# Scores, decay, rate and gate as plain 32-bit products on half the array's height, in a hybrid attention and RWKV layer

## Chip, cores, metric

The kernel runs on one core of one Trainium2 chip. The metric is device time in microseconds for one launch. The core's engines are TensorE (PE, with its weight loads as PEld), VectorE (DVE), ScalarE (ACT), GpSimd (POOL) and SyncE (SP, which issues most DMAs). Every engine works through its own instructions in order and waits on semaphores for the others.

## What is computed

One decoder layer on 512 positions with 16 learned positions ahead of them (528 in all), width 1024, all in 32 bits. After a layer norm, one projection gives the inputs of two branches and their gates. One branch is attention over a sliding window of 128 positions with 16 query heads and 2 key heads of width 64; the other is a recurrent time mixing (RWKV-7) with 16 heads. The parts of the reference that the change touches:

```python
proj = h @ w_in[l]
q, k, v, zr, gate_att, gate_rwkv = jnp.split(proj, [c0, c1, c2, c3, c4], axis=-1)
...
logits = jnp.einsum('nqkgd,nskd->kgnqs', qb, kw).astype(jnp.float32) * (HEAD_DIM ** -0.5)
...
w = -jax.nn.softplus(-(w0 + jnp.tanh(wl) @ w2)) - 0.5      # decay
a = jax.nn.sigmoid(a0 + al @ a2)                           # rate
g = jax.nn.sigmoid(gl) @ g2                                # output gate
...
merged = jax.nn.sigmoid(gate_att) * att + jax.nn.sigmoid(gate_rwkv) * rw
h = layer_norm(ALPHA * h + merged @ w_out[l], ln1_g[l], ln1_b[l])
ff = jnp.square(jax.nn.relu(h @ w_ff1[l])) @ w_ff2[l]
h = layer_norm(ALPHA * h + ff, ln2_g[l], ln2_b[l])
```

`decay_w2` and `iclr_a2` have 64 rows, `gate_w2` 128; a head's query and key have width 64, so the scores are sums over 64 values.

## The kernel before

Activations lie with channels on the 128 partitions and positions along the free dimension. A large product is made of split operands: a 32-bit number x becomes a high part hi (rounded to the type fp32r) and a low part lo = x - hi. ACT makes hi by a copy, DVE makes lo by a subtraction (`split`, lines 256 and 259, for weights), and the helper `three` (lines 339 to 342) adds hi·hi, hi·lo and lo·hi into one PSUM bank.

The first 560 us or so interleave the two branches; then follow the output projection and the two feed-forward products. The heads go in 8 pairs (index j), each on 128 partitions, 64 for each head. Two kinds of work are woven on TensorE. A *unit* is a column block of the projection, made by `dense` in steps (8 steps of 512 positions, or 16 of 264), each step three products. All else is an *item* with a due time. `weave` keeps a clock that each dense step advances by a fixed estimate, 3 x (0.014 + n / 2400) us for n positions (0.372 for 264, 0.682 for 512; line 371), and puts an item into TensorE's order as soon as the clock has reached its time. TensorE's order is fixed by this; the other engines' orders come from the framework's scheduler with priorities (`ahead`). Stage s of the loop at line 1447 scans pair s, solves pair s - 1, projects decay and rate of pair s + 1 (`project_in`, items at 7.4 and 8.6), makes the scores of pair s - 1 (`attend`) and the attention output of pair s - 2. In the middle stages the units are the two gates (512 positions each), then keys and reads (264), the query (512) and the values (264).

Around the change:

- `low_rank` and `gate_rank` make the shared inputs: `zw` and `za` hold hi on partitions 0 to 63 and lo on 64 to 127 for decay and rate; `sghi` and `sglo` hold the gate's.
- `rwkv_begin` loads a pair's 64-row weights of decay and rate, laid out twice, below each other, and splits them. `rwkv_lora(j, 0)` makes decay for both halves of the positions and `rwkv_lora(j, 1)` the rate: for each half one product with the weights' hi (against hi and lo of the input at once, 128 rows) and one with lo. Each half takes one PSUM bank and is read by a tanh on ACT (line 500). After decay follow a scan on DVE (line 505) and exponentials on ACT (lines 512 to 516), which the pair's keys use.
- `aside_query` splits the query (`qhi` by ACT, line 1073; `qlo` by DVE, line 1074) and moves the parts by four DMAs into `qs`, with hi and lo of one head below each other. `aside_key` and `aside_heads` do the like for the key, with each head's hi twice, and lo twice.
- `attention_scores(j, n)` makes the scores of query block n of 128 against 256 keys for both heads in one bank: two products for each head, with the key's hi and lo. DVE then merges the window's two halves and adds the bias (lines 1140, 1141). It is called four times for a pair, at t0, t0, t0 + 2.8 and t0 + 4.4, and the last call also does the softmax.
- `gate_out` makes the output gate with `three`; DVE multiplies it into the other gate (line 1126).

Small products such as decay and rate, gate, scores, and the softmax's transposes (`pt`) and attention output (`av`) share the PSUM pool `pat` with two banks, used in turn; the dense steps have another with two banks (`dn`).

Other small products already take plain 32-bit operands: `rwkv_scores` (line 668) and `rwkv_fold` (line 890) use 64 rows, one head after the other on the two halves of the array; `rwkv_turn_inverse` (line 873) uses all 128 rows; the chain of states (line 950) uses all rows and half of the columns. On the planner's clock `rwkv_fold` has its items at 8.4 and 10.6, `rwkv_turn_inverse` at 6.4, the chain one each 0.95 from 11.6, `gate_out` 11.6.

Of the kernel before, what the change touches and what calls it, by code (L numbers as in the profile page):

```python
# [11 lines left out]
F32 = mybir.dt.float32  # L12
# [72 lines left out]
ABUF = {'qs': 1, 'ga': 1, 'gg': 1, 'pa': 1, 'z': 1, 'bv': 1}  # L85
# [45 lines left out]
def hybrid_layer_kernel(ctx: ExitStack, tc: tile.TileContext, I: dict, out: bass.AP):  # L131
# [298 lines left out]
    zw = lz.tile([P, T], F32R, name="zw", tag="zw")  # L430
    za = lz.tile([P, T], F32R, name="za", tag="za")
    sghi = lz.tile([P, SEQ], F32R, name="sghi", tag="sghi")
    sglo = lz.tile([P, SEQ], F32R, name="sglo", tag="sglo")
# [11 lines left out]
    def low_rank(zl):  # L445
        twl = ew.tile([HD, T], F32, name="twl", tag="u")
        act.activation(twl, zl[0:HD], AF.Tanh)
        tal = ew.tile([HD, T], F32, name="tal", tag="L")
        act.copy(tal, zl[HD:P])
        for dst, src in ((zw, twl), (za, tal)):  # L450
            act.copy(dst[0:HD], src)
            dve.tensor_tensor(dst[HD:P], src, dst[0:HD].bitcast(F32), op=ALU.subtract)

    def gate_rank(zg):
        sg = ew.tile([P, SEQ], F32, name="sg", tag="v")
        act.activation(sg, zg[:, NMETA:], AF.Tanh, scale=0.5)
        dve.tensor_scalar(sg, sg, 0.5, 0.5, op0=ALU.mult, op1=ALU.add)
        act.copy(sghi, sg)
        dve.tensor_tensor(sglo, sg, sghi.bitcast(F32), op=ALU.subtract)
# [16 lines left out]
    def rwkv_begin(j):  # L476

        S = SS[j]
        lw = ew.tile([P, 2, P], F32, name="lw", tag="lw")
        lhi = ew.tile([P, 2 * P], F32R, name="lhi", tag="lhi")  # L480
        llo = ew.tile([P, 2 * P], F32R, name="llo", tag="llo")
        lf = lw.rearrange("p a c -> p (a c)")
        nc.sync.dma_start(lf, I["lora"][j])
        act.copy(lhi, lf)
        dve.tensor_tensor(llo, lf, lhi.bitcast(F32), op=ALU.subtract)
        S["lora"] = lhi, llo
# [3 lines left out]
    def rwkv_lora(j, q):  # L490
        S = SS[j]
        lhi, llo = S["lora"]
        zz, dst, bias = ((zw, S["tw"], "w0h"), (za, S["ta"], "a0h"))[q]
        qc = slice(q * P, (q + 1) * P)
        for t0, n in ALLT:
            ps = pat.tile([P, 512], F32, name="dps", tag="a")
            ts_ = slice(t0, t0 + n)
            pe.matmul(ps[:, :n], lhi[:, qc], zz[:, ts_], start=True, stop=False)
# [1250 lines left out]
```

## Time and profile before

| | |
|---|---|
| median of 3 runs | 990.89 us (987.24 to 992.4) |
| profiled execution: its time, its span | 988.82 us, 986.7 us |
| mean granted clock of TensorE | 0.994 |
| PE, PEld | 943.9, 790.8 us busy |
| DVE, ACT, POOL | 654.9, 455.0, 45.9 us busy |
| DMA | 105.46 MB, mean 107 GB/s |

The profile is of one execution. In the timeline a row is start (us), duration (us), engine, line, operation, tiles written<-read, rows*columns of the array for TensorE, shapes, and in brackets the idle time ahead of it with what ended it. TensorE's products overlap, so that their durations (0.28 us for 264 columns) exceed the distance of their starts (0.12 us); what a product costs is that distance. A 32-bit product appears as two instructions. Group rows give busy us, mean ns, and after the bar the idle time before them.

### The profile page before, as it was taken

What the parts mean: (1) busy time and instruction counts of PE and PEld (TensorE: products, weight loads), DVE (VectorE), ACT (ScalarE), POOL (GpSimd) and SP (SyncE); (2) the same over time, 40 slices, a digit from 0 to 9 for tenths busy, and PEclk for the clock granted to TensorE, in tenths of its full rate; (3) what the DMA queues carried; (4) which work ended last, traced back from release to release, by engine and by line L of the source; (5) the groups of instructions that cost most, each with busy time, mean ns of one, the idle gap of its engine ahead of it and who ended that gap; (6) DMA issues with size and microseconds to landing.
All of it is one profiled execution on the core that took longest, in us unless ns stands there. A gap on an engine that the chain in (4) does not pass through costs nothing.

```text
span 986.7 us, 19121 instructions
## 1 busy us (share of the span) xinstructions
PE 943.9 (96%) x7557; PEld 790.8 (80%) x7557; DVE 654.9 (66%) x1505; ACT 455.0 (46%) x1130; POOL 45.9 (5%) x108
## 2 busy tenths in 40 slices
PE   4999999999999999999999999999999999999996
PEld 3889878788888887888876778888888888888885
DVE  8677887888887888778786967666523244452427
ACT  6635447465473664654726834644412133442220
POOL 2000000010010000100001001000000000000001
PEclk9999999999999999999999999999999999999998
DMA  7545323233324432242534536133232323223222
GB/s 272 95 131 150 90 73 105 82 77 98 91 74 120 105 98 59 69 111 80 147 116 105 194 114 228 44 122 113 89 103 86 106 86 104 89 88 104 76 96 85
DMA packets 82673, 105.46 MB, mean 107 GB/s; under 512 B 47766, under 2 KB 54664, under 8 KB 82584
## 3 DMA queue, kind: packets, MB, share of 16 engines
q1 hardware_dynamic: 81088, 102.16, 35.0%
q10 hardware_dynamic: 1496, 2.08, 0.6%
q8 instruction: 59, 0.97, 0.4%
q14 instruction: 30, 0.25, 0.1%
HBM read 86.29 MB, written 13.74 MB: 101 GB/s over the span
## 4 chain that ended last, share of the span: by engine, by line
PE 72%; DVE 16%; ACT 5%; DMA 3%; issue 2%; POOL 2%; SPq 0%; DVEq 0%; ACTq 0%; POOLq 0%
PE dps L340 12%; PE dps L341 11%; PE dps L342 11%; PE acc L1518 6%; PE acc L1520 6%; PE acc L1519 6%; DVE wlo L259 3%; DMA wraw<-in_w_in_dram 2%; PE sc L668 2%; PE o L1292 1%; PE av L1196 1%; PE wp L873 1%; POOL grs L973 1%; PE ch L950 1%; PE o L1293 1%
## 5 line engine op out<-in xcount | busy, mean ns | idle before, releaser
L259 DVE TENSOR_TENSOR wlo<-wraw,whi 128x512 fp32r<-128x512 f32 x240 | 158.4, 686 | 178.2 <-ACT whi L256 177.4
L256 ACT CAST whi<-wraw 128x512 fp32r<-128x512 f32 x240 | 140.5, 616 | 271.8 <-PE dps L341 131.2
L340 PE MATMUL dps<-hhi,whi 128*128 128x264 f32 (+1 forms) x640 | 217.7, 340 | 7.3 <-DVE qlo L1074 5.5
L341 PE MATMUL dps<-hlo,whi 128*128 128x264 f32 (+1 forms) x640 | 204.5, 320 | 1.1 <-DVE hlo L321 1.1
L342 PE MATMUL dps<-hhi,wlo 128*128 128x264 f32 (+1 forms) x640 | 204.1, 319 | 0.4 <-DVE wlo L259 0.4
L340 PEld LDWEIGHTS dps<-hhi,whi 128*128 128x128 f32 x640 | 121.5, 190 | 22.2 <-DVE qlo L1074 6.8
L342 PEld LDWEIGHTS dps<-hhi,wlo 128*128 128x128 f32 x640 | 121.4, 190 | 9.1 <-DVE wlo L259 0.6
L341 PEld LDWEIGHTS dps<-hlo,whi 128*128 128x128 f32 x640 | 121.8, 190 | 7.3 <-DVE hlo L321 1.9
L341 PE MATMUL dps<-h1lo,whi 128*128 128x512 f32 (+1 forms) x256 | 97.5, 381 | 0.0
L340 PE MATMUL dps<-h1hi,whi 128*128 128x512 f32 (+1 forms) x256 | 97.5, 381 | 0.0
L342 PE MATMUL dps<-h1hi,wlo 128*128 128x512 f32 (+1 forms) x256 | 97.5, 381 | 0.0
L341 PEld LDWEIGHTS dps<-h1lo,whi 128*128 128x128 f32 x256 | 48.1, 188 | 10.2
L342 PEld LDWEIGHTS dps<-h1hi,wlo 128*128 128x128 f32 x256 | 48.1, 188 | 10.2
L340 PEld LDWEIGHTS dps<-h1hi,whi 128*128 128x128 f32 x256 | 48.1, 188 | 10.2
L1518 PE MATMUL acc<-whi,hhi 128*128 128x512 f32 x128 | 50.6, 395 | 0.0
L1519 PE MATMUL acc<-wlo,hhi 128*128 128x512 f32 x128 | 50.4, 394 | 0.0
L1520 PE MATMUL acc<-whi,hlo 128*128 128x512 f32 x128 | 50.2, 392 | 0.0
L1520 PE MATMUL acc<-whi,flo 128*128 128x512 f32 x112 | 44.0, 393 | 0.0
L1518 PE MATMUL acc<-whi,fhi 128*128 128x512 f32 x112 | 43.8, 391 | 0.0
L1519 PE MATMUL acc<-wlo,fhi 128*128 128x512 f32 x112 | 43.8, 391 | 0.0
L908 ACT ACTIVATE Z<-ch,PC 64x64 f32<-64x64 f32 x56 | 17.4, 310 | 41.0 <-PE ch L950 40.5
L1618 DVE TENSOR_TENSOR rl<-rl 128x512 f32<-128x512 f32 (+1 forms) x36 | 22.8, 632 | 15.2 <-ACT hhi L1617 9.1
(302 smaller groups left out, 1732.6 us busy)
## 6 DMA issues: line engine op xcount, KB each, us to landing
wraw<-in_w_ff_dram SPq DMA_DIRECT2D x64, 512.0 KB, 3.5
wraw<-in_w_in_dram SPq DMA_DIRECT2D x52, 512.0 KB, 3.6
wraw<-in_w_out_dram SPq DMA_DIRECT2D x8, 512.0 KB
xt<-in_x_dram SPq DMA_DIRECT2D x4, 512.0 KB, 7.5
Nd<-NT SPq DMA_DIRECT2D x16, 128.0 KB, 3.0
bv<-bv SPq DMA_DIRECT2D x8, 256.0 KB, 2.1
bvm<-bv SPq DMA_DIRECT2D x8, 256.0 KB
qs<-qhi SPq DMA_DIRECT2D x16, 128.0 KB, 2.2
```

Of the source, the lines that this page charges most:

```text
L256: act.copy(hi[:n, qs], raw[:n, qs])
L259: dve.tensor_tensor(lo[:n, qs], raw[:n, qs], hi[:n, qs].bitcast(F32), op=ALU.subtract)
L340: pe.matmul(ps, whi, xhi, start=first, stop=False)
L341: pe.matmul(ps, whi, xlo, start=False, stop=False)
L342: pe.matmul(ps, wlo, xhi, start=False, stop=last)
L668: pe.matmul(scs[e][:, c * P : (c + 1) * P], BK[ER[e], 4 * i + c, :], AXg[ER[e], e, 4 * i + c], start=True, stop=True,)
L873: pe.matmul(w4[:, c, :], XB[:, 4 * i + c, :], S["AT"][:, 4 * i + c, :], start=True, stop=True,)
L908: act.activation(dst, src[e][ER[e]], AF.Copy, scale=scale)
L1518: pe.matmul(acc[b], xhi[k][:, bs], hi[:, ws], start=first, stop=False)
L1519: pe.matmul(acc[b], xhi[k][:, bs], lo[:, ws], start=False, stop=False)
L1520: pe.matmul(acc[b], xlo[k][:, bs], hi[:, ws], start=False, stop=last)
L1618: dve.tensor_tensor(r, r, r, op=ALU.mult)
```

## The change

The scores, decay and rate, and the output gate take their operands as plain 32-bit numbers. `zz` holds the decay's input on partitions 0 to 63 and the rate's on 64 to 127, the pair's weights of decay lie above those of the rate in one 128x128 tile, and `rwkv_lora(j, q)` now does one half of the positions (264) for both: two products of 64 rows, one on each half of the array's height, into two banks. The decay's scan follows the second call. The query is one tile, copied by ACT only, and the key one tile with its 64 rows twice; the DMAs of the query's parts are gone. `attention_scores(j, i)` does two query blocks, with one bank for each head: four products of 64 rows and 256 columns, the heads in turn. It is called twice for a pair, at t0 and t0 + 3.6. The gate is one product of 128 rows and 512 columns. The first feed-forward weights, which reuse tiles that have become free, reuse `zz`, `sg`, `kk` and `q`. Dense units are as before. The diff, without its context:

```diff
-ABUF = {'qs': 1, 'ga': 1, 'gg': 1, 'pa': 1, 'z': 1, 'bv': 1}
+ABUF = {'q': 2, 'ga': 1, 'gg': 1, 'pa': 1, 'z': 1, 'bv': 1}
...
-    zw = lz.tile([P, T], F32R, name="zw", tag="zw")
-    za = lz.tile([P, T], F32R, name="za", tag="za")
-    sghi = lz.tile([P, SEQ], F32R, name="sghi", tag="sghi")
-    sglo = lz.tile([P, SEQ], F32R, name="sglo", tag="sglo")
...
+    zz = lz.tile([P, T], F32, name="zz", tag="zz")
+    sg = lz.tile([P, SEQ], F32, name="sg", tag="sg")
...
     def low_rank(zl):
-        twl = ew.tile([HD, T], F32, name="twl", tag="u")
-        act.activation(twl, zl[0:HD], AF.Tanh)
-        tal = ew.tile([HD, T], F32, name="tal", tag="L")
-        act.copy(tal, zl[HD:P])
-        for dst, src in ((zw, twl), (za, tal)):
-            act.copy(dst[0:HD], src)
-            dve.tensor_tensor(dst[HD:P], src, dst[0:HD].bitcast(F32), op=ALU.subtract)
+        act.activation(zz[0:HD], zl[0:HD], AF.Tanh)
+        act.copy(zz[HD:P], zl[HD:P])
...
     def gate_rank(zg):
-        sg = ew.tile([P, SEQ], F32, name="sg", tag="v")
...
-        act.copy(sghi, sg)
-        dve.tensor_tensor(sglo, sg, sghi.bitcast(F32), op=ALU.subtract)
...
-        lw = ew.tile([P, 2, P], F32, name="lw", tag="lw")
-        lhi = ew.tile([P, 2 * P], F32R, name="lhi", tag="lhi")
-        llo = ew.tile([P, 2 * P], F32R, name="llo", tag="llo")
-        lf = lw.rearrange("p a c -> p (a c)")
-        nc.sync.dma_start(lf, I["lora"][j])
-        act.copy(lhi, lf)
-        dve.tensor_tensor(llo, lf, lhi.bitcast(F32), op=ALU.subtract)
-        S["lora"] = lhi, llo
+        S["lora"] = lw = ew.tile([P, P], F32, name="lw", tag="lw")
+        nc.sync.dma_start(lw, I["lora"][j])
...
     def rwkv_lora(j, q):
-        S = SS[j]
-        lhi, llo = S["lora"]
-        zz, dst, bias = ((zw, S["tw"], "w0h"), (za, S["ta"], "a0h"))[q]
-        qc = slice(q * P, (q + 1) * P)
-        for t0, n in ALLT:
-            ps = pat.tile([P, 512], F32, name="dps", tag="a")
-            ts_ = slice(t0, t0 + n)
-            pe.matmul(ps[:, :n], lhi[:, qc], zz[:, ts_], start=True, stop=False)
-            pe.matmul(ps[:, :n], llo[:, qc], zz[:, ts_], start=False, stop=True)
...
+        S = SS[j]
+        t0, n = ALLT[q]
+        ts_ = slice(t0, t0 + n)
+        outs = (S["tw"], "w0h"), (S["ta"], "a0h")
+        pss = [pat.tile([P, 512], F32, name="lps", tag="a") for e in range(2)]
+        for e in range(2):
+            pe.matmul(
+                pss[e][:, :n], S["lora"][ER[e]], zz[ER[e], ts_], start=True, stop=True
+            )
+        for ps, (dst, bias) in zip(pss, outs):
...
-        if q == 0:
-            tw = dst
+        if q == 1:
+            tw = S["tw"]
...
-    kd = dr.tile([2, P, T], F32, name="kd")
+    kd = dr.tile([P, T], F32, name="kd")
...
     def aside_key():
-        hi = at.tile([P, T], F32R, name="khi_", tag="sph")
-        lo = at.tile([P, T], F32R, name="klo_", tag="spl")
+        t = lz.tile([P, T], F32, name="ka", tag="q", bufs=ABUF["q"])
...
         def evict(ps, t0, n):
-            ts_ = slice(t0, t0 + n)
-            act.copy(hi[:, ts_], ps[:, :n])
-            dve.tensor_tensor(lo[:, ts_], ps[:, :n], hi[:, ts_].bitcast(F32), op=ALU.subtract)
+            act.copy(t[:, t0 : t0 + n], ps[:, :n])
...
         def after():
-            nc.sync.dma_start(kd[0], hi.bitcast(F32))
-            nc.sync.dma_start(kd[1], lo.bitcast(F32))
+            nc.sync.dma_start(kd, t)
...
     def aside_value():
-        t = at.tile([P, T], F32, name="va", tag="sph")
+        t = lz.tile([P, T], F32, name="va", tag="q", bufs=ABUF["q"])
...
-        khi = at.tile([P, NK], F32R, name="khi", tag="khi")
-        klo = at.tile([P, NK], F32R, name="klo", tag="klo")
-        pool.memset(khi[:, 0:PADK].bitcast(F32), 0.0)
-        pool.memset(klo[:, 0:PADK].bitcast(F32), 0.0)
-        nc.sync.dma_start(khi[0:64, PADK:].bitcast(F32), kd[0, R])
-        nc.sync.dma_start(khi[64:128, PADK:].bitcast(F32), kd[0, R])
-        nc.sync.dma_start(klo[0:64, PADK:].bitcast(F32), kd[1, R])
-        nc.sync.dma_start(klo[64:128, PADK:].bitcast(F32), kd[1, R])
...
+        kk = lz.tile([P, NK], F32, name="kk", tag="kk")
+        pool.memset(kk[:, 0:PADK], 0.0)
+        for e in range(2):
+            nc.sync.dma_start(kk[ER[e], PADK:], kd[R])
...
-        A["khi"], A["klo"], A["vT"] = khi, klo, vT
+        A["kk"], A["vT"] = kk, vT
...
     def aside_query(j):
-        hi = at.tile([P, T], F32R, name="qhi", tag="sph")[:, :SEQ]
-        lo = at.tile([P, T], F32R, name="qlo", tag="spl")[:, :SEQ]
+        q = lz.tile([P, T], F32, name="q", tag="q", bufs=ABUF["q"])[:, :SEQ]
...
-                act.activation(hi, ps, AF.Copy, scale=HD**-0.5)
-                dve.scalar_tensor_tensor(
-                    lo, ps, HD**-0.5, hi.bitcast(F32), op0=ALU.mult, op1=ALU.subtract
-                )
-            qs = [
-                at.tile([P, SEQ], F32R, name=f"qs{e}", tag=f"qs{e}", bufs=ABUF["qs"])
-                for e in range(2)
-            ]
-            for e in range(2):
-                for d, src in enumerate((hi, lo)):
-                    nc.sync.dma_start(
-                        qs[e][64 * d : 64 * d + 64].bitcast(F32),
-                        src[64 * e : 64 * e + 64].bitcast(F32),
-                    )
-            A["qs", j], A["bias", j] = qs, bias
+                act.activation(q, ps, AF.Copy, scale=HD**-0.5)
+            A["q", j], A["bias", j] = q, bias
...
-        gw = at.tile([P, P], F32, name="gw", tag="gw")
-        gwh = at.tile([P, P], F32R, name="gwh", tag="gwh")
-        gwl = at.tile([P, P], F32R, name="gwl", tag="gwl")
+        gw = at.tile([P, P], F32, name="gw", tag="gw", bufs=2)
...
-        act.copy(gwh, gw)
-        dve.tensor_tensor(gwl, gw, gwh.bitcast(F32), op=ALU.subtract)
...
-        A["gw", j] = gwh, gwl
+        A["gw", j] = gw
...
-        three(gp, *A["gw", j], sghi, sglo)
+        pe.matmul(gp, A["gw", j], sg, start=True, stop=True)
...
-    def attention_scores(j, n):
-        khi, klo, qs, bias = A["khi"], A["klo"], A["qs", j], A["bias", j]
-        if n == 0:
+    def attention_scores(j, i):
...
+        kk, q, bias = A["kk"], A["q", j], A["bias", j]
+        if i == 0:
...
-        sp = pat.tile([P, 512], F32, name="sp", tag="a")
-        s3 = sp.rearrange("p (e s) -> p e s", e=2)
+        sps = [pat.tile([P, 512], F32, name="sp", tag="a") for e in range(2)]
+        for d in range(2):
+            n = 2 * i + d
+            for e in range(2):
+                pe.matmul(
+                    sps[e][:, d * 256 : (d + 1) * 256], q[ER[e], n * P : (n + 1) * P],
+                    kk[ER[e], n * P : n * P + 256], start=True, stop=True,
+                )
...
-            win = slice(n * P, n * P + 256)
-            blk = slice(n * P, (n + 1) * P)
-            pe.matmul(s3[:, e], qs[e][:, blk], khi[:, win], start=True, stop=False)
-            pe.matmul(s3[:, e], qs[e][:, blk], klo[:, win], start=False, stop=True)
-        dve.copy_predicated(s3[:, :, P:], later, s3[:, :, 0:P])
-        dve.tensor_tensor(sb[:, n], s3[:, :, P:], bias, op=ALU.add)
-        if n == 0:
+            s3 = sps[e].rearrange("p (n s) -> p n s", n=2)
+            dve.copy_predicated(s3[:, :, P:], later, s3[:, :, 0:P])
...
-                sb[:, n], sb[:, n], cv("pad1").unsqueeze(1).to_broadcast([P, 2, P]), op=ALU.add
+                sb[:, 2 * i : 2 * i + 2, e], s3[:, :, P:],
+                bias[:, e].unsqueeze(1).to_broadcast([P, 2, P]), op=ALU.add,
...
-        if n < 3:
+        if i == 0:
+            dve.tensor_tensor(
+                sb[:, 0], sb[:, 0], cv("pad1").unsqueeze(1).to_broadcast([P, 2, P]), op=ALU.add
+            )
...
-            [lz.tile([P, SEQ], F32R, name="w1", tag=t) for t in tags]
-            for tags in (("zw", "za"), ("sghi", "sglo"))
+            [lz.tile([P, SEQ], F32R, name="w1", tag=t, bufs=ABUF.get(t, 1)) for t in tags]
+            for tags in (("zz", "sg"), ("kk", "q"))
...
     def attend(j, t0):
-        return [(t0, (f"q{j}",), F(attention_scores, j, 0))] + [
-            (t0 + t, (), F(attention_scores, j, 1 + i)) for i, t in enumerate((0.0, 2.8, 4.4))
+        return [
+            (t0, (f"q{j}",), F(attention_scores, j, 0)), (t0 + 3.6, (), F(attention_scores, j, 1)),
...
-    lora = np.stack([a["decay_w2"][0], a["iclr_a2"][0]], 1).reshape(HD, 2, PAIRS, P)
-    lora = lora.transpose(2, 0, 1, 3).reshape(PAIRS, HD, 2 * P)
+    lora = np.concatenate([a["decay_w2"][0], a["iclr_a2"][0]], 0)
...
-        "lora": np.concatenate([lora, lora], 1),
+        "lora": lora.reshape(P, PAIRS, P).transpose(1, 0, 2),
```

## Prediction

> **What bounds the kernel now.** I read the page first: its busy time and the chain that ended last.
>
> ```profile
> span 986.7 us, 19121 instructions
> PE 943.9 (96%) x7557; PEld 790.8 (80%) x7557; DVE 654.9 (66%) x1505; ACT 455.0 (46%) x1130; POOL 45.9 (5%) x108
> PE 72%; DVE 16%; ACT 5%; DMA 3%; issue 2%; POOL 2%; SPq 0%; DVEq 0%; ACTq 0%; POOLq 0%
> ```
>
> TensorE (PE) is busy for 96% of the span and carries 72% of the chain. So work taken from VectorE (DVE), ScalarE (ACT) or the DMA queues is worth only what TensorE waits for them, and work added to TensorE counts in full. The second view is therefore the waits of TensorE alone: who is waited for, total us, times, longest.
>
> ```profile
> PE dps L340 <- DVE qlo L1074: 5.5, 6, 0.9
> PE sp L1138 <- ACT ta L500: 2.7, 4, 0.7
> PE sp L1138 <- DVE sb L1141: 1.8, 1, 1.8
> PE vp L1054 <- issue: 1.5, 1, 1.5
> PE vp L1054 <- ACT ta L500: 1.5, 1, 1.5
> PE dps L498 <- DVE zw L452: 1.4, 1, 1.4
> PE dps L340 <- ACT whi L256: 1.1, 1, 1.1
> PE sp L1138 <- DMA qs<-qlo: 0.7, 1, 0.7
> PE dps L342 <- DVE wlo L259: 0.4, 1, 0.4
> ```
>
> The split operands stand behind most of these lines: the query's low part (qlo), the copies of it (qs), the low-rank input (zw), and the late reading of the rate's banks (ta). Without the two rows of the weights' split they are 15.1 us. The question is whether the new products cost TensorE more than what goes of these 15.1 us. The third view is the timeline of TensorE in one middle stage (start, duration, instruction); the prices come from differences of starts, since durations overlap.
>
> ```profile
> 187.08 0.39 PE L342 MATMUL dps<-hhi,wlo 128*128 128x512 f32 x1
> 187.32 1.95 PE L873 MATMUL wp<-AT,XB 128*128 128x128 f32 x16
> ...
> 194.08 0.39 PE L498 MATMUL dps<-za,lhi 128*128 128x264 f32 x1
> 194.31 0.29 PE L499 MATMUL dps<-za,llo 128*128 128x264 f32 x1
> ...
> 194.67 0.39 PE L340 MATMUL dps<-hhi,whi 128*128 128x512 f32 x1
> ...
> 195.14 0.40 PE L342 MATMUL dps<-hhi,wlo 128*128 128x512 f32 x1
> 196.21 0.38 PE L1138 MATMUL sp<-khi,qs 128*128 128x256 f32 x1 [0.68 <-ACT ta L500]
> ...
> 196.55 0.28 PE L1138 MATMUL sp<-khi,qs 128*128 128x256 f32 x1
> ...
> 197.14 0.28 PE L1139 MATMUL sp<-klo,qs 128*128 128x256 f32 x1
> ...
> 198.43 0.39 PE L342 MATMUL dps<-hhi,wlo 128*128 128x512 f32 x1
> 198.75 1.16 PE L890 MATMUL gq<-GR,WT 64*128 64x128 f32 x16
> 199.84 0.39 PE L340 MATMUL dps<-hhi,whi 128*128 128x264 f32 x1
> 200.07 0.29 PE L341 MATMUL dps<-hlo,whi 128*128 128x264 f32 x1
> 200.20 0.28 PE L342 MATMUL dps<-hhi,wlo 128*128 128x264 f32 x1
> ...
> 201.04 0.50 PE L340 MATMUL gp<-sghi,gwh 128*128 128x512 f32 x1
> ...
> 201.84 0.28 PE L340 MATMUL dps<-hhi,whi 128*128 128x264 f32 x1
> ```
>
> **Prices on TensorE.** From 194.31 to 194.67 three products of 264 columns take 0.36 us, 0.12 each; from 196.55 to 197.14 five of 256 columns take 0.59 us, 0.12 each. The full-height 32-bit product of line 873 has a row among the groups by form:
>
> ```profile
> L873 PE MATMUL wp<-AT,XB 128*128 128x128 f32 x128 | 15.6, 275 | 0.0
> ```
>
> It is two instructions per product (16 for eight), each (1.95 - 0.275) / 15 = 0.11 us at 128 columns. Two dense products of 512 columns take 0.47 us (194.67 to 195.14), 0.23 each; with 0.12 for 264 that is 0.43 ns a column, and 0.11 us is twice 128 columns. So a plain 32-bit product costs four column times, two in each instruction: 0.22 us an instruction at 256 columns, 0.227 at 264, 0.44 at 512.
>
> Line 890 is what the change uses: 64 rows, two halves of the array in turn, eight products, 16 instructions. From 198.75 to 199.84 it takes 1.09 us, not 16 x 0.11 = 1.8, so two run side by side. But such a visit also costs at its edges. The dense product ahead of it lasts 0.32 us instead of 0.23 (198.43 to 198.75), the one behind it 0.23 instead of 0.13 (199.84, 200.07, 200.20). Line 873, full height, makes the product ahead of it last 0.24 us, nearly nothing: the edge belongs to the change of height, not to 32 bits. Inside, 1.09 us is nine slots of 0.112 us and 0.08 us. The nine rather than eight I take from the chain's visit, with half the columns and two products:
>
> ```profile
> 143.80 0.34 PE L950 MATMUL ch<-Z,AX 128*64 128x64 f32 x4
> 144.07 0.39 PE L340 MATMUL dps<-hhi,whi 128*128 128x264 f32 x1
> ```
>
> 0.27 us is three slots of 0.056 us and 0.10 us, so n products in turn make n + 1 slots with a nearly constant rest of 0.10; with n slots the rests would be 0.16 and 0.19. A visit of its own thus costs (n + 1) slots and 0.29 us of edges (0.09 ahead, 0.10 inside, 0.10 behind).
>
> **Added on TensorE, part by part.**
> Scores: 2 visits for each of 8 pairs, 4 products of 256 columns each: 5 x 0.22 + 0.29 = 1.39 us, 16 visits 22.2 us. Today it is 16 products of 0.12 for each pair, at 0.119 us 15.2 us in all, and no edges, since they have the dense products' height. +7.0 us.
> Decay and rate: 2 products in a visit, 16 visits. Ten stand alone (the first of each pair, and the second of pairs 0 and 1, whose stages have no fold next to them): 3 x 0.227 + 0.29 = 0.97 us. Six follow a fold's visit of the same height in the same step (8.4 and 8.6 on the planner's clock) and add two slots, 0.45 us; the edge behind the fold is paid today too (0.23 us, 194.08 to 194.31). 9.7 + 2.7 = 12.4 us against 64 x 0.122 = 7.8. +4.6 us.
> Gate: one full-height product of 512 columns, 2 x 0.44 + 0.10 = 0.98 us, against 0.80 us from 201.04 to 201.84 for three. +0.18 x 8 = +1.4 us.
> Sum: +13.0 us. Nothing hides it, TensorE being the bound.
>
> **What goes of the waits.** The order in ACT explains the second row of waits.
>
> ```profile
> 194.32 0.22 ACT L512 ACTIVATE Pm<-L 128x16 f32<-128x16 f32 x1 [1.32 <-DVE L L505]
> 195.68 0.84 ACT L500 ACTIVATE ta<-dps,drv 128x264 f32<-128x264 f32 x2
> ```
>
> Today decay's two tanh run early, its scan follows on DVE, and the exponentials queue in ACT ahead of the rate's tanh, whose banks the scores need. In the changed order both evictions of a visit come right behind it, at about 194.65 and, with 0.84 us for two, done by 195.5, while TensorE comes to the scores at 195.5. The wait goes: 0.84 us (1.07 from 195.14 to 196.21 against 0.23) and 0.10 of refill, four times: -3.8 us. The two transposes of values (vp) need one bank and follow at once; of 1.63 us each (1.5 idle and the refill) about 0.55 stays, the time of the first tanh: -2.2 us. What moves later by some 2.7 us is the scan and the exponentials. Queued behind them on ACT are the next casts of weights and the gate's tanh; their users are the keys, one unit later, so I cost it at nothing; if that cover is gone it costs a wait like the present 0.84 us a stage.
>
> ```profile
> 166.70 0.60 ACT L1073 ACTIVATE qhi<-dps 128x512 fp32r<-128x512 f32 x1
> 167.35 0.69 DVE L1074 SCALAR_TENSOR_TENSOR qlo<-dps,qhi 128x512 fp32r<-128x512 f32 x1
> 168.09 0.39 PE L340 MATMUL dps<-hhi,whi 128*128 128x264 f32 x1 [0.92 <-DVE qlo L1074]
> ```
>
> The bank of the query is now free at 167.30, when ACT ends, instead of 168.04. Next late is ACT itself, so 0.74 of each wait goes: 6 x 0.74 = -4.4 us. It could be all of it if the copy comes earlier in ACT's order, and nothing if later.
>
> ```profile
> 32.59 0.63 ACT L449 COPY tal<-k 64x528 f32<-64x528 f32 x1
> 33.91 0.70 DVE L452 TENSOR_TENSOR zw<-twl,zw 64x528 fp32r<-64x528 f32 x1 [1.49 <-ACT zw L451]
> ```
>
> The low-rank input is ready at 33.22 instead of 34.61: -1.4 us. The wait for the query's copies (0.7 idle, 0.8 with refill) has no DMA left to wait for: -0.8 us; SP's queue loses those 32 issues and issues the weights behind them earlier, which no wait of TensorE asks for. The 1.8 us before the last pair's scores is a conflict for two banks with the transposes of the softmax; the new order has it too, with the scores first. I take half, -1.0 us, between 0 and 1.8. The key's low part goes from a full DVE ahead of the late casts (1.1 and 0.4 us): -0.4 us, between 0 and 1.5. Sum: -14.0 us.
>
> **Balance:** +13.0 - 14.0 = -1.0 us on the profiled execution's 988.8 us, so 987.8. The median of the three runs, 990.9, is 2.1 us above it; on that footing 989.9 us.
>
> **Rivals.**
> A, no odd slot. TensorE: Matmul & The Clock Gate of the Trainium skill (Measured speedup vs the span model) gives packed tiles the time of one product and about 4 ns for each further tile. The rests above speak, weakly, for the slot. By n slots a visit of scores is 4 x 0.22 + 0.19 + 0.19 = 1.26 us, one of decay and rate 0.83: 16 x 0.13 + 10 x 0.14 = 3.5 us less, 986.4 us. Still within 0.5%.
> B, the relief goes further. Each pair loses several splits on DVE and ACT; if ACT copies the query before TensorE is there (2.0 us more), the transposes' banks come free in time (1.1), and the last pair's conflict (0.8) and the late casts (1.1) vanish, it is 5.0 us more: 984.9 us. For it: those engines are where all these rows end. Against it: ACT takes work in order, and the cast ahead of the query's copy waits for a DVE product that stays.
> C, slower: both banks at once. A visit of scores now takes both banks of its PSUM pool together, and its second half needs the one that the gate's product holds. That is read by
>
> ```profile
> 202.69 0.67 DVE L1126 SCALAR_TENSOR_TENSOR gg<-gg,gp 128x512 f32<-128x512 f32 x1
> ```
>
> done at 203.36, 1.5 us after the product's end. The second visit would come near 204.9. The later scan and exponentials fall into this stretch; if they push this reading by over 1.5 us, each second visit waits, say one such DVE instruction, 8 x 0.67 = 5.4 us, and the first visits keep their 3.8: +9.2, 999.1 us. Against it: the evictions stand ahead in program order.
> D, the halves don't run side by side at these widths: 16 x 3 x 0.22 + (10 + 12) x 0.227 = 15.6 us more, 1005.5 us. Line 890 speaks against it.
>
> **How the numbers follow.** A measurement of this kernel can tell about 0.5%, 5 us, from no change (the three runs span 987.24 to 992.4). Forecast 0.31 (its own range 986 to 994), A 0.11, B 0.29, C 0.22, D 0.07. Faster is B, 0.29; the same is forecast and A, 0.42; slower is C and D, 0.29. The range reaches from B with A's slots, 981.4, to just past C, 999.5, and leaves out D.
>
> **What would show it.** Right: no row for qlo, zw or ta ahead of scores in TensorE's waits; the row of the query's bank now names ACT and about 0.2 us each; visits of scores of 1.2 us with a longer product on each side; gate products of 0.9 us; TensorE's span outside waits up by some 13 us. Wrong: scores' visits under 1.1 or over 1.8 us inside (A, D), new waits for the scores' or the gate's readers (C), or a sum of TensorE's waits down by over 17 us (B).

## The result and the profile after

| | before | after |
|---|---|---|
| median of 15 runs each | 986.52 us (984.7 to 992.4) | 983.63 us (982.03 to 985.52) |
| ratio of the runs, 95% interval | | 0.9963 [0.9949, 0.9977] |
| profiled execution: its time, its span | 988.82, 986.7 us | 983.9, 982.1 us |
| forecast on each footing | | 987.8 profiled; 989.9 on the median of three |

By the ratio of the runs the change makes the kernel 0.37% faster (0.23 to 0.51%), within 0.5% as the forecast and its rival A have it; between the two medians it is -2.9 us, 0.29%. The forecast itself, -1.0 us, is 1.9 us short of that. Of all runs one, of the kernel of experiment 3, took 1813.56 us and is left out of the ratios. The page after:

```profile
span 982.1 us, 18960 instructions
PE 949.9 (97%) x7549; PEld 778.5 (79%) x7549; DVE 646.1 (66%) x1476; ACT 447.5 (46%) x1111; POOL 45.5 (5%) x106
PE 74%; DVE 16%; ACT 3%; DMA 2%; issue 2%; POOL 2%; SPq 0%; DVEq 0%; POOLq 0%; ACTq 0%
```

TensorE is busy 6.0 us longer, every other engine less, and the span is still shorter: busy time was exchanged for waits, as the prediction describes. TensorE's waits after (who is waited for, total us, times, longest):

```profile
PE pt L1144 <- DVE sb L1107: 1.6, 1, 1.6
...
PE dps L340 <- DVE k L415: 1.3, 1, 1.3
PE dps L340 <- ACT q L1052: 1.2, 6, 0.2
PE axt L695 <- DVE AX L882: 1.1, 4, 0.3
PE dps L340 <- ACT whi L256: 1.0, 1, 1.0
PE ch L937 <- DVE Z L893: 0.8, 2, 0.7
PE vp L1034 <- ACT tw L487: 0.7, 1, 0.7
PE vp L1034 <- issue: 0.6, 1, 0.6
...
PE dps L342 <- DVE wlo L259: 0.2, 1, 0.2
```

The rows of qlo, ta, zw and qs are gone. The query's bank is now held by ACT (1.2 in place of 5.5 us), the values' transposes (vp) wait 1.3 in place of 3.0. Two rows are new: axt, the turning of the fold's sums, and k. One stayed under another name: the last pair's conflict, 1.8 us on the scores before, is 1.6 us on the softmax's transposes (pt). Without the two waits at the very start, the list falls from 22.8 to 12.3 us, by 10.5.

**Where the time went, stage by stage.** A stage is counted from the first product wp to the next stage's. Two short stretches have to be set apart first. In windows of 1 us, the last column but two being TensorE's granted clock, the profile of before shows

```profile
131.00:132.00 1.00, 1.00 (x7) 1.00 (x7) 0.59 (x4) 0.29 (x1) 0.00 (x0) 0.59 0.22 66
132.00:133.00 1.00, 1.00 (x5) 0.90 (x4) 1.00 (x6) 0.00 (x0) 0.00 (x0) 0.50 0.20 66
133.00:134.00 1.00, 1.00 (x4) 0.71 (x4) 1.00 (x5) 0.00 (x0) 0.00 (x0) 0.50 0.00 0
134.00:135.00 1.00, 1.00 (x5) 0.48 (x5) 0.05 (x1) 0.38 (x1) 0.00 (x0) 0.71 0.00 0
```

TensorE is busy throughout, but the clock is halved for 3.4 us, which costs 0.41 + 0.50 + 0.50 + 0.29 = 1.7 us. Before has two such dips (here and at 73 to 77 us), after has one (26 to 30 us). Setting 1.7 us apart for each, the spans are 983.3 and 980.4 us: -2.9 us.

One profile of each kernel cannot say how often dips come, but the other runs have their mean granted clock on record. It is 0.9952 on average in the 45 runs of before that stand beside the experiments, 21 of them below 0.996, and 0.9973 in the 15 of after, none below. The difference, 0.0021 of a span, is 2.1 us, of the 3.8 us by which the mean spans of these runs differ. At the same granted clock (0.996, 0.997, 0.998) the spans of before are 2.2, 1.4 and 2.2 us longer. So some 2 us of the gain are the kernel's own at an equal clock, and about as much goes with the clock. That the removed waits are what spares the dips is not shown.

| stretch | before, us | after, us | difference |
|---|---|---|---|
| to the first stage (a dip each taken off) | 120.15 | 119.19 | -0.96 |
| stage 1 (before: a dip taken off) | 63.78 | 63.54 | -0.24 |
| stages 2, 3, 4 | 63.76, 63.75, 63.75 | 64.01, 63.94, 64.01 | +0.70 in all |
| stage 5 | 65.38 | 64.64 | -0.74 |
| stages 6 and 7 | 64.11, 59.87 | 64.02, 59.85 | -0.11 |
| output projection, feed-forward, end | 418.73 | 417.20 | -1.53 |

The seven stages that hold most of the change give 0.4 us, and the middle ones became longer. About half of the 2.9 us lies in the last row, where the products are the same, 1.0 us of it here:

```profile
712.20:978.60 266.40, 266.40 (x1152) 216.15 (x1151) 106.58 (x166) 71.70 (x126) 2.77 (x3) 1.00 0.28 92
```

```profile
708.90:974.30 265.40, 265.40 (x1153) 215.84 (x1151) 106.55 (x166) 71.49 (x126) 2.77 (x3) 1.00 0.29 92
```

These are the windows of before and after over the last 1152 products, the second feed-forward product in two halves and part of the first between them: busy without a gap at full clock in both, 1.0 us apart. By differences of starts nearly all of it lies in the four blocks of 96 products that read the tiles `fhi` and `flo`: they take 21.9 to 22.0 us each before and 21.5 to 21.8 after, all other blocks the same to 0.02 us. This length goes with the kernel: 266.4 in before and in its variant below, 265.4 to 266.0 in the kernels with plain decay and rate, 265.2 in those with split decay and rate beside plain scores. So does the whole last row, with 418.7 and 418.2, 416.6 to 417.2, and 415.2 to 415.3 us. Why is open; differences of 1 to 3 us between the kernels below have this part in them.

### The profile page after: what moved, and what is told of

Same layout as the page of the kernel before. It is cut to its first block, busy times and chain, and to the rows that moved or that the text cites. A ratio compares the mean times of both kernels' runs of the same rounds, so it can differ in the third digit from the quotient of the medians.

```text
span 982.1 us, 18960 instructions
## 1 busy us (share of the span) xinstructions
PE 949.9 (97%) x7549; PEld 778.5 (79%) x7549; DVE 646.1 (66%) x1476; ACT 447.5 (46%) x1111; POOL 45.5 (5%) x106
## 4 chain that ended last, share of the span: by engine, by line
PE 74%; DVE 16%; ACT 3%; DMA 2%; issue 2%; POOL 2%; SPq 0%; DVEq 0%; POOLq 0%; ACTq 0%
PE dps L340 13%; PE dps L341 11%; PE dps L342 11%; PE acc L1486 6%; PE acc L1487 6%; PE acc L1488 6%; DVE wlo L259 2%; PE o L1260 2%; PE av L1164 2%; PE sc L655 2%; PE o L1261 1%; PE o L1262 1%; DVE Xf L766 1%; POOL grs L960 1%; DVE ftmp L762 1%
## 5 line engine op out<-in xcount | busy, mean ns | idle before, releaser
L340 PE MATMUL dps<-hhi,whi 128*128 128x264 f32 (+1 forms) x640 | 222.6, 348 | 3.5 <-DVE k L415 1.3
```

What stands on the lines that cost most here:

```text
L340: pe.matmul(ps, whi, xhi, start=first, stop=False)
```

## The experiments

All ratios are to the kernel before. "Expected" was written before the run.

**1. The scores alone as before** (split halves of query and key, their copies and four products; the rest as changed).

```diff
-                pe.matmul(
-                    sps[e][:, d * 256 : (d + 1) * 256], q[ER[e], n * P : (n + 1) * P],
...
+            pe.matmul(s3[:, e], qs[e][:, blk], khi[:, win], start=True, stop=False)
+            pe.matmul(s3[:, e], qs[e][:, blk], klo[:, win], start=False, stop=True)
```

> The changed kernel with the scores alone as before (split query and key, four visits a pair); decay, rate and gate stay plain. Theory, a sum of two sides: against the changed kernel TensorE gets back 5.0 us (16 visits of 1.26 us against 15.2 us for the split products), and the waits for the query come back (5.5 instead of 1.2 us for the bank, 0.7 for the copies), 5.1 us with refill. So within 1.5 us of the changed kernel: ratio to before 0.995 to 0.998. Rival, relief: the whole gain is the unloading of DVE and ACT, most of it by the query; then at least 4 us slower than the changed kernel, ratio 1.000 or more.

Measured: 982.2 us, ratio 0.9944 [0.9927, 0.996]. The waits of TensorE:

```profile
PE dps L340 <- DVE qlo L1061: 5.6, 6, 0.9
...
PE sp L1121 <- DVE sb L1124: 2.1, 1, 2.1
PE ch L937 <- DVE Z L893: 1.9, 5, 0.6
```

The wait for qlo is back in full, the one for axt is gone, and a middle stage is 63.75 instead of 63.94 us, the length of before. So by the stages the plain scores don't pay inside this change: the 0.7 us that they buy at the query's bank is less than what they cost a middle stage on TensorE and at axt. The intervals of the two ratios overlap. Beside split decay and rate it is otherwise (experiment 11). The result lies just under the range that was expected, far from the rival's.

**2. Decay and rate alone as before** (split weights and inputs, first the decay's two products, then the rate's).

```diff
-            pe.matmul(
-                pss[e][:, :n], S["lora"][ER[e]], zz[ER[e], ts_], start=True, stop=True
-            )
...
+            pe.matmul(ps[:, :n], lhi[:, qc], zz[:, ts_], start=True, stop=False)
+            pe.matmul(ps[:, :n], llo[:, qc], zz[:, ts_], start=False, stop=True)
```

> The changed kernel with decay and rate alone as before (split operands, decay whole first, then the rate). Theory of two sides: TensorE gets back 3.3 us, but the waits for the rate's banks (2.7 and 3.0 us idle against 1.3 now) and for the low-rank input (1.4) come back, 7 us with refill: 3 to 4 us slower than the changed kernel, ratio to before 0.999 to 1.001. Rival: these waits were only exchanged for others, and TensorE's 3.3 us decide: ratio 0.992 to 0.994.

Measured: 983.83 us, 0.9965 [0.9949, 0.998]. Both lost; the result is that of the whole change. The waits of TensorE:

```profile
PE vp L1044 <- ACT ta L497: 3.0, 2, 1.5
PE sp L1110 <- ACT ta L497: 2.7, 4, 0.7
```

They are those of before to the tenth. What TensorE saves and what axt no longer waits is just what these rows cost: a middle stage is 63.97 beside 63.94 us.

**3. The gate alone as before.**

```diff
-        pe.matmul(gp, A["gw", j], sg, start=True, stop=True)
+        three(gp, *A["gw", j], sghi, sglo)
```

> The changed kernel with the gate alone as before (three split products, low and high parts of input and weights by ACT and DVE). Theory: TensorE gets back 0.17 us for each of 8 pairs, 1.3 us, and no wait depended on these splits: ratio to before 0.994 to 0.996. Rival, relief: the splits on ACT and DVE cost as much as TensorE gains: no faster than the changed kernel, 0.9963 or more.

Measured: 983.21 us, 0.9953 [0.9934, 0.9972]. TensorE's waits name axt again:

```profile
PE axt L699 <- DVE AX L886: 1.9, 5, 0.4
```

The ratio is in the expected range, but the stages are not: the gate's products are 0.17 us cheaper a stage, and the wait for axt behind them grew from 1.1 to 1.9 us; the middle stages stay at 63.95.

**4. The two halves of the scores one after the other in program order** (both products of the first head, then both of the second).

```diff
-        for d in range(2):
-            n = 2 * i + d
-            for e in range(2):
+        for e in range(2):
+            for d in range(2):
+                n = 2 * i + d
```

> The changed kernel with one edit: in a visit of the scores both query blocks of the first head come ahead of both of the second, instead of the heads in turn. Theory: a visit is n pairs of instructions side by side plus fixed edges of 0.39 us. Out of turn the halves don't overlap except where the heads meet: up to 3 or 4 more slots of 0.216 us in each of 16 visits, 10 to 14 us slower than the changed kernel, ratio to before 1.007 to 1.011; visits of 1.7 to 1.9 us instead of 1.06. Rival: overlap does not depend on the order of the products, ratio 0.996.

Measured: 983.67 us, 0.9959 [0.9942, 0.9977]. The theory fell:

```profile
201.35 1.14 PE L1100 MATMUL sp<-kk,q 64*128 64x256 f32 x8
202.42 0.39 PE L340 MATMUL dps<-hhi,whi 128*128 128x264 f32 x1
```

The timeline gives 1.07 us for the visit, as in the changed kernel (1.06). The two starts of a pair lie 13 ns apart instead of 7. Here it does not matter which half's products stand first: they overlap all the same.

**5. Both heads on the first half** (the second head's products read the first 64 rows, so its scores are those of other data).

```diff
-                    sps[e][:, d * 256 : (d + 1) * 256], q[ER[e], n * P : (n + 1) * P],
-                    kk[ER[e], n * P : n * P + 256],
+                    sps[e][:, d * 256 : (d + 1) * 256], q[ER[0], n * P : (n + 1) * P],
+                    kk[ER[0], n * P : n * P + 256],
```

> The changed kernel with all four products of a scores' visit on the first 64 rows of the array; it leaves out the second head's scores, which are taken from the first head's query and key. Theory, two halves side by side, each with its own queue of products: nothing is left to share, a visit has 8 slots of 0.216 us instead of 4, about 1.9 us instead of 1.06, and the kernel is some 14 us slower (about 997 us against 983.6). Rival: a 32-bit product of 64 rows costs half of a full-height one by itself, whatever its partner: visits of 1.06 us, time as the changed kernel.

Measured in one run: 992.5 us, span 990.7. The visit in the timeline:

```profile
204.49 1.99 PE L1100 MATMUL sp<-kk,q 64*128 64x256 f32 x8
206.41 0.39 PE L340 MATMUL dps<-hhi,whi 128*128 128x264 f32 x1
```

It takes 1.92 us: eight slots of 0.216 and 0.19. On two halves it is 1.06, four slots and 0.20. So the two halves work side by side, and the second one is free to the slot. The total is between the two expectations: 16 x 0.86 = 13.7 us more on TensorE made the profiled span 8.6 us longer. A middle stage grew by 0.95, not 1.71 us; the wait for axt is not in this kernel's list.

**6. Decay's scan as an item of its own, later on the planner's clock.**

```diff
+            (13.2, (), F(rwkv_decay, j)),
```

> The changed kernel with decay's scan and exponentials as an item of their own at 13.2 on the planner's clock, behind the evictions of the scores and the fold's sums; products unchanged. Theory: the new wait of the transposes axt for the fold's sums (0.28 us idle and 0.4 us of delay around it, in four stages) comes from the scan, which moved into a stretch where DVE has no gap; then the wait goes and the middle stages fall from 63.94 to about 63.3 us, ratio to before 0.993 to 0.995. Rival: TensorE has merely come nearer to a DVE that is full there anyway: the wait stays and the stage keeps 63.9.

Measured: 981.81 us, 0.9951 [0.9934, 0.9967]. The expected ratio, but not for the expected reason. The scan on DVE and the wait of TensorE, in that order:

```profile
192.84 1.25 DVE L495 TENSOR_TENSOR_SCAN L<-con,tw 128x528 f32<-128x528 f32 x1
...
PE axt L698 <- DVE AX L885: 1.1, 4, 0.3
```

The stage begins at 182.83, so the scan stands 10.01 us into it; in the changed kernel (below) it is 194.44 - 184.45 = 9.99. The edit did not move it, and axt waits as before. What went is the wait for the query's copy, 0.2 us in 6: on ACT that copy now follows the cast of rk at once (289.87 after 289.23), where a weight's cast stood between (291.93, then 292.57). The stage is 0.46 us shorter, as much as the pause at that copy was longer than a product (0.48 us between starts against 0.12, and 0.11 behind it). As a test of the scan it failed.

**7. Before, with the products of decay and rate in the halves' order** (all operands split; only the order of products and evictions as in the change).

```diff
-        for t0, n in ALLT:
+        t0, n = ALLT[q]
+        for e in range(2):
...
+        for ps, (_, dst, bias) in zip(pss, outs):
```

> The kernel before with one edit: decay and rate, still as split products, are made by halves of the positions (both for the first half at 7.4, both for the second at 8.6) instead of decay whole and then the rate. Theory: the wait of the scores for the rate's banks is a matter of this order and not of the plain operands, so it goes (0.94 us in middle stages, 1 us or more in the two with the values' transposes), and the late scan brings the axt wait (0.6): middle stages 63.4 us instead of 63.75, ratio 0.995 to 0.998. Rival: the plain form is what removes the wait: 63.75, ratio 1.000.

Measured: 984.85 us, 0.9972 [0.9961, 0.9983], as expected; but the wait that came is not the expected one for axt. The row of ta is gone without any plain product. With it go 0.8 us in stage 1 (63.02 us against 63.8 without the dip) and 0.8 in stage 5. A middle stage gains only 0.2 us (63.58), because DVE is met elsewhere, in the chain's step ch:

```profile
PE dps L340 <- DVE qlo L1076: 5.5, 6, 0.9
PE ch L952 <- DVE Z L908: 3.7, 6, 0.9
```

**8. The change, with decay and rate split but in the halves' order.** The diff is that of 2 with the loop of 7.

> The changed kernel with decay and rate as split products but in the changed order by halves. Theory: the plain products cost TensorE 0.34 us a stage more than these, which comes back, unless the axt wait takes it as it seems to have taken the gate's 0.17: middle stages 63.6 to 63.9 us, the wait for the low-rank input (1.4 us at the start) back, ratio 0.995 to 0.997. Rival: the split work on ACT and DVE (casts and differences of weights, 0.8 us a stage) delays evictions: over 63.94 and ratio over 0.997.

Measured: 979.5 us, 0.9926 [0.991, 0.9942]; a middle stage 63.44 us. That is better than expected. Beside experiment 2 only the order differs: 0.0039 of the ratio, 3.8 us. Beside the change itself only the plain products: without them it is 0.0037 faster, 3.6 us (each interval is some 1.6 us wide to either side). In the profiles the seven stages are 3.4 us shorter (0.4 to 0.75 in each of six, nothing in the last), the stretch ahead of them 0.7 longer and the last row 2.0 shorter. TensorE's price for the plain products, 3.4 us over the 16 visits (worked out below), is of the size of what the stages give. Beside plain scores, the order was the gain of this part and the plain operands its cost.

**9. The turning of the folded sums later**, behind the scores' second visit.

```diff
-            (12.4, (), F(rwkv_turn_scores, j)),
+            (13.0, (), F(rwkv_turn_scores, j)),
```

> The changed kernel with one number other: the turning of the folded sums (the tile axt) is asked for at 13.0 us of a stage in place of 12.4, which puts it behind the second visit of the scores on TensorE, where it stands in the kernel before. Theory (the turn is asked for before VectorE has added the fold's second sums): the wait axt <- DVE AX (1.1 us in 4) goes from the waits, the visit of axt falls from 1.01 to 0.79 us and the stall of 0.34 us ahead of it goes, so that a middle stage falls from 63.9 to 63.3-63.6 us; ratio to the kernel before 0.992 to 0.995. Rival (the time only moves: what the transposed sums feed is then late, or the scores' own bank): a stage keeps 63.9 us, ratio 0.995 to 0.998, and a new wait of as much stands in the waits.

Measured: 981.36 us, 0.9942 [0.9918, 0.9966]. By its ratio the theory holds, by its stages the rival: 63.95 us. The waits and one place of the timeline:

```profile
PE ch L937 <- DVE Z L893: 3.7, 7, 0.7
...
199.44 0.34 PE L937 MATMUL ch<-Z,AX 128*64 128x64 f32 x4 [0.70 <-DVE Z L893]
```

The wait for axt has become a wait of the chain, whose Z DVE computes right behind those sums. The row of q is gone too, and the stage is no shorter for it. The ratio's gain lies elsewhere, stages 1, 5 and 7 being shorter by 0.3, 0.3 and 0.6 us.

**10 to 12. Combinations:** 8 with 9; 8 with a split gate; 8 with 9 and 6.

> Decay and rate with split operands in the halves' order (as in lora_split_halves, scores and gate plain), and the turning of the folded sums at 13.0 in place of 12.4. Theory: the two repairs are independent, so the 0.14 us stall and the 0.22 us inside axt's visit come off each middle stage: 63.44 to 63.0-63.2 us, ratio 0.990 to 0.992. Rival: with the split products the sums are in time already (no wait on AX stands in that kernel's list), the ratio stays 0.992 to 0.994.

> Only the scores as plain 32-bit products; decay, rate and gate with split operands, decay and rate in the halves' order. Theory (the gate's plain products cost TensorE 0.2 us a stage, and nothing waits for the gate's splits): a middle stage falls by 0.1 to 0.2 us beside lora_split_halves (63.44), to 63.25-63.35; ratio 0.991 to 0.9925. Rival (the gain runs into the wait for the folded sums, as it did in gate_split): stages stay at 63.4 us, ratio 0.9925 to 0.994.

> halves_axt with decay's scan and exponentials listed as an item of their own at 13.2 us of the stage. In scan_later this item left the scan where it was on VectorE, but on ScalarE it put the query's copy ahead of a weight's cast, and the wait dps <- ACT q (0.2 us in 6) was gone, 0.46 us a stage. Theory (that wait comes from ScalarE's order alone): the same here, wherever the order comes out so, and the ratio is 0.986 to 0.990. Rival (the order comes out otherwise beside these products): the wait stays and the ratio is that of halves_axt, 0.990 to 0.992.

Measured: 978.83 us, 0.9911 [0.9885, 0.9937]; 978.93 us, 0.9913 [0.9887, 0.994]; 978.81 us, 0.9915 [0.9882, 0.9949]. All three beat both kernels (the third's interval touches that of the change), and none can be told from the others or from experiment 8. In the first and third the middle stage is 63.73 and 63.64 us, longer than the 63.44 of 8, against both theories; stages 1, 5 and 7 make up for it. In the third the wait for q is gone, as in the first, and the stage is no shorter for it. With the gate split the stage is 63.42 us, as its rival has it (the ratio lies in the theory's range). The wait for axt is back,

```profile
PE axt L711 <- DVE AX L898: 1.0, 4, 0.3
```

so what TensorE saves at the gate it spends there.

Experiments 7 and 11 differ by the scores alone (with query and key), split in the one and plain in the other: 0.9972 and 0.9913, 5.8 us, with intervals that lie apart. So the plain scores pay beside split decay and rate, though not in the whole change. In the profiles only 1.8 us of it lie in the stages, 1.1 ahead of them and 3.0 in the last row, whose lengths are unexplained.

## Why the prediction was right, and where it was not

**The step that was mis-sized: n + 1 slots.** Visits of scores and of decay and rate with dense products on both sides, in the timeline after:

```profile
123.15 0.40 PE L342 MATMUL dps<-hhi,wlo 128*128 128x512 f32 x1
123.48 0.72 PE L483 MATMUL lps<-zz,lw 64*128 64x264 f32 x4
124.12 0.50 PE L340 MATMUL dps<-hhi,whi 128*128 128x512 f32 x1
...
202.26 0.28 PE L342 MATMUL dps<-hhi,wlo 128*128 128x264 f32 x1
202.48 1.14 PE L1100 MATMUL sp<-kk,q 64*128 64x256 f32 x8
203.54 0.39 PE L340 MATMUL dps<-hhi,whi 128*128 128x264 f32 x1
203.77 0.28 PE L341 MATMUL dps<-hlo,whi 128*128 128x264 f32 x1
```

Scores: 203.54 - 202.48 = 1.06 us inside, 0.10 ahead (0.22 for a product of 0.12) and 0.10 behind: 1.26, not 1.39. Decay and rate: 0.64 inside, 0.85 with edges, not 0.97. Those are nearly rival A's figures, 1.26 and 0.83: n slots and a constant of 0.2 inside. The prediction had this reading before it (rests of 0.16 and 0.19) and took the smoother fit of two visits instead of the sizes that it gave. The rule of the Trainium skill that rival A rests on (TensorE: Matmul & The Clock Gate, Measured speedup vs the span model) agrees: the pair costs one product, as experiment 5 shows to the slot. Its 4 ns for a further tile is of the size of the 6 to 7 ns between the two starts of a pair, but it counts a product's duration, not the distance of starts, and gives no figure for the 0.2 us inside a visit nor for the edges. For the edges, TensorEngine Tiling (Array Packing) of the Trainium skill, Key Properties, says that changing the tiling mode drains TensorE, without a price; the trace agrees, with some 0.1 us on each side.

TensorE's additions are then: scores 16 x 1.26 - 15.2 = +5.0 us (predicted +7.0); decay and rate 10 x 0.85 and six behind a fold at 0.45 (0.54 in the records, of which the fold's own visit saves 0.09), less 7.8 = +3.4 (predicted +4.6); the gate +1.3 (predicted +1.4), its price having moved into the product behind it:

```profile
197.95 1.12 PE L1086 MATMUL gp<-sg,gw 128*128 128x512 f32 x2
198.52 0.69 PE L340 MATMUL dps<-hhi,whi 128*128 128x264 f32 x1
199.04 0.28 PE L341 MATMUL dps<-hlo,whi 128*128 128x264 f32 x1
```

0.57 from gp to the dense product, and 0.52 to the next where 0.12 is its own. In all +9.7 instead of +13.0, near rival A's sum (+9.5).

**The waits: right where they were named, too good in sum.** Taken off as forecast: the wait for ta (the order does it, experiment 7), zw, qs, and qlo (5.5 to 1.2 us; the pause at the query's bank, measured between starts, fell from 1.20 to 0.49, 0.71 of the 0.74). The values' transposes keep 0.65 us each (0.55 forecast). Not taken off: the last pair's conflict, forecast to halve, keeps 1.6 of 1.8 us; the late casts 1.2 of 1.5. Added, where the prediction put what the later scan delays at nothing: a wait for the fold's sums. In the changed kernel DVE shows

```profile
194.44 1.25 DVE L492 TENSOR_TENSOR_SCAN L<-con,tw 128x528 f32<-128x528 f32 x1
...
198.46 0.69 DVE L259 TENSOR_TENSOR wlo<-wraw,whi 128x512 fp32r<-128x512 f32 x1 [0.20 <-ACT whi L256]
199.06 0.38 DVE L767 COPY Xr<-Xf 64x256 f32<-64x256 f32 x1
199.38 1.27 DVE L882 TENSOR_TENSOR AX<-AX,gq 128x512 f32<-128x512 f32 x2
```

and TensorE

```profile
195.66 1.16 PE L877 MATMUL gq<-GR,WT 64*128 64x128 f32 x16
196.75 0.39 PE L340 MATMUL dps<-hhi,whi 128*128 128x264 f32 x1
...
199.53 0.29 PE L342 MATMUL dps<-hhi,wlo 128*128 128x264 f32 x1
200.10 1.25 PE L695 MATMUL axt<-con,AX 128*128 128x128 f32 x8 [0.28 <-DVE AX L882]
201.11 0.37 PE L340 MATMUL dps<-hhi,whi 128*128 128x264 f32 x1
```

The fold's products are over at about 196.8, but their sums start on DVE at 199.38, 2.6 us later. TensorE is ready for them at 199.65 (199.53 and 0.12), stands until 200.10, and again inside axt (to 201.11, 1.01 us; before it is 0.79):

```profile
203.04 1.03 PE L708 MATMUL axt<-con,AX 128*128 128x128 f32 x8
203.83 0.37 PE L340 MATMUL dps<-hhi,whi 128*128 128x264 f32 x1
```

That is 0.67 us in each of four stages, 2.7 us. The prediction asked whom the later scan would make wait and named the keys' users and, in rival C, the gate's reader; the row that appeared is that of the fold's sums. That the scan alone is the cause is not shown, since experiment 6 didn't move it, but the kernels together say how far it can be. From the end of the fold's products to the second pair of sums, in the first middle stage:

| kernel | scan, us into the stage | delay of the sums, us |
|---|---|---|
| before (all split) | 5.7 | 0.6 |
| experiment 7 (all split, halves' order) | 9.3 | 1.8 |
| experiment 2 (plain scores and gate, old order) | 5.7 | 1.35 |
| experiment 8 (plain scores and gate, halves' order) | 9.3 | 2.35 |
| the change | 10.0 | 2.55 |

So the halves' order, which makes the scan late, goes with 1.0 to 1.2 us of the delay, the plain scores and gate with 0.6 to 0.8, and the plain decay and rate with 0.2. Which of DVE's instructions does it stays open. Experiments 3 and 9 show that DVE is what TensorE meets here, whichever product comes next.

**Balance.** The forecast counted each wait with the refill behind it, so idle time alone (-10.5 us) is too little to set against it. Between starts, from 24.3 us, where both kernels start the same product, to the end of stage 7, with the dips set apart, TensorE's pauses at waits fell from 28.4 to 16.1 us, -12.3, and all other intervals grew by 11.0: the 9.7 above and 1.3 inside axt. That is -1.3, what the table has for the stages and the stretch ahead of them (-1.35). (Up to 20 us after was 0.6 us ahead, because its clock went full at 19.5 instead of 21.95 us; by 24 us that is gone.) Against the forecast, TensorE is 3.3 us too much, and the waits, with the 1.3 inside axt, are -11.0 instead of -14.0. By luck the two errors took each other out: -1.0 is a good figure reached by two wrong ones. Rival A had TensorE right, and its -4.5 us is the forecast without that luck. The rest of the 2.9 us is the 1.5 us of the last row, which no step had, and what the runs gain by their clock no step had either. B's further relief didn't come; what C feared, a late reader on DVE, came in another place at less than a third of its price; D fell with experiment 5. The footing was off too: the median of three runs stood 4.4 us above that of fifteen, and the profiled execution 2.3 above it, with its two dips.

## What to carry to other kernels

A change that does two things should be priced as two: here, beside plain scores, the order of products and evictions won 3.8 us and the plain operands of decay and rate cost 3.6. Such prices hold for their surroundings: the plain scores gained 5.8 us beside split decay and rate and nothing to be seen beside plain ones. A wait removed on the bounding engine is worth its length only if the next operand is already there: where VectorE is full for 10 us, cheaper or later products were met by it in another row of the waits. And before stages of two profiles are subtracted, look at the granted clock in fine windows, and compare the mean clock of all runs: one dip of 3.4 us cost 1.7 us, more than any stage gained.

## What the runs showed of the hardware

Two products on the two halves of the array's rows overlap fully at 256 columns (1.06 us for four pairs, 1.92 us for eight on one half), whether they stand in turn or in a row. A visit costs about 0.2 us beyond its slots inside and 0.1 us on each side, at 128 columns (1.09 us for eight slots of 0.112) as at 256 and 264.

The clock dips were not expected: full clock, 3.4 us at 0.50, full clock again, in stretches where TensorE is busy. The profiles of all kernels together have ten of them ahead of TensorE's last product, and each begins at most 1.6 us behind the last of waits of TensorE that are 0.9 to 2.1 us in all (two begin 0.1 to 0.2 us before that wait's end): the one shown behind 1.5 us for vp, the one of after behind two of 0.7 us for hlo. Not every such wait brings one: the same wait for vp in stage 5 of before, and those of after, brought none. In the trace's own record of the clock its changes lie whole multiples of 3.413 us apart (in before 51.20, 3.41, 54.61 and 3.41 us, in after 6.83 and 3.41), and every dip lasts one of them. So it seems that a wait can cost 1.7 us beyond its length, and that it hangs on where in these windows it falls; what decides it is open. That a kernel with fewer waits has fewer dips is not shown, though the runs of after have fewer (the clock of 0.9973 against 0.9952). TensorE: Matmul & The Clock Gate of the Trainium skill (Part 1: The HAM clock gate) describes half or full clock set by a free-running activity window of about 3.4 us, low after an idle window; the depth and the length agree, but no wait ahead of a dip is as long as a window (the longest is 2.1 us), so less than an idle window was enough.
